# A decoder trunk with product-key experts on one core: more buffers for the gathered v rows

## The chip, the cores and the metric

The kernel runs on one core of a Trainium2 chip. The metric is device time in microseconds of one execution. The runs shown are 1572.21, 1564.13 and 1569.64 us, with a median of 1569.64 us.

## The reference, cut to what matters

The layer has an attention and a recurrent half, and then a product-key expert layer (PEER). Each of 256 tokens picks 16 experts in each of 8 heads out of 16,384. Expert e has a row u[e] and a row v[e], each of 2048 floats:

```
experts = i1 * N_KEYS + i2                       # (token, head, k)
g = softmax(best_s)
act = gelu(einsum('chkd,cd->chk', u_tab[experts], xc))
out = einsum('chk,chkd->cd', g * act, v_tab[experts])
y = rmsnorm(h + out, final_norm_g)
```

## The kernel before, in words

The expert layer is computed densely over u and sparsely over v.

**u stretch.** All 16,384 u rows are multiplied with all tokens; the activations x of the tokens, split in a high and a low part, lie in the tile `xc` (32 KB on each of the 128 partitions). For every expert the activations of the 256 tokens go to a table in DRAM, `wg_d`, and the gates are added there by indirect DMAs (`scatter`, L701). While this runs, VectorE and TensorE make lists of the experts that were picked by at least one token.

**v stretch** (`b_stage`). The picked experts are worked off in 109 tiles of 128 experts. The first two (kind BO) are loaded directly, 107 are gathered: `gather_w` (L895) fetches 128 rows of the table (1 or 2 KB a row, tile `wg`), `gather_v` (L886) fetches the 128 rows of v (8 KB a row, 1 MB in all, tile `vr`). Both are indirect DMAs on GpSimd's queue, in one order. For every tile `ready` makes the weights (`split_w`, VectorE L907 or L909 and what follows it) and splits the v rows into a high part on ScalarE (`vh`, L935 or L938) and a low part on VectorE (`vl`, L936 or L939), in halves of 1024 columns; `multiply` (L951) adds the products of 512 columns into eight PSUM banks. A tile's kind says which token halves it serves: S0 and S1 (one expert of each row used once, so the weight is put into v as a factor: L909, L918, L938, L939) take 8 products, DO 16 (it splits v twice: L907, L912, four L938 and four L939), M0 and M1 12, BO 24 (L907, L935, L936). The kinds are spread evenly; tiles 54 to 64 are DO, S1, BO, BO, M1, S0, S1, BO, M0, DO, BO.

**Buffers.** `vr` and `wg` have five buffers each. In iteration i the program asks for `gather_w(i + 5)`, `gather_v(i + 5)`, `ready(i + 2)` and `multiply(i)`. `gather_v(i + 5)` needs the buffer of tile i, which is free when the split of tile i is done; `gather_w(i + 5)` needs the buffer that `split_w(i)` has read. `vh` and `vl` have eight half buffers each, four tiles of a kind other than DO.

**Order.** A planner puts the instructions of each engine into a fixed order beforehand, by priority (the place in the program) and by when it expects inputs and buffers to be there, so an engine's order is not the program's line by line. A data-dependent branch (`leftovers`, not taken) stands after iteration 1.

**End.** The tile `fin` takes over the place of `xc`: the first four of its 512-column blocks hold the final gain row (`load_fg`, L966), four take the output of token half 0 and four that of half 1. `residual` (L970, SyncE's queue) and `add_residual` add the residual during iterations 4 to 82.

Of the kernel before, what the change touches and what calls it, by code (L numbers as in the profile page):

```python
# [9 lines left out]
F32 = mybir.dt.float32  # L10
# [10 lines left out]
D = 2048  # L21
# [29 lines left out]
ONCE = (S0, DO, S1)  # L51
NT = 107
AHEAD = 5
LOOK = 2
NLEAD = 3
NS1 = 1
# [7 lines left out]
def trunk_kernel(ctx, tc, hT_d, par_d, sink_d, fg_d, win_d, wr_d, wi_d, wout_d, wq_d, sk_d, u_d, v_d, out_d):  # L64
# [31 lines left out]
    box = {}  # L96
# [5 lines left out]
    def at(slot, fn):  # L102
        later.setdefault(slot, []).append(fn)
# [755 lines left out]
    def close_a():  # L859
        ps_x.close()  # L860
        box["bx"] = ExitStack()
        pob = box["bx"].enter_context(tc.tile_pool(name="pob", bufs=1, space=PSUM, reuse_waits="tile"))
        box["o"] = [[pob.tile([128, 512], F32, name=f"oacc{tb}_{q}") for q in range(4)] for tb in range(2)]
        fin = box["xpool"].tile([128, 12, 512], F32, tag="xc", name="fin")
        box["fin"], box["fin2"] = fin[:, 0:8, :], fin[:, 8:12, :]

    tail = [(M1, BASES[M1] + CAPS[M1] - 1 - i) for i in range(3)]
# [4 lines left out]
    order = [(BO, None)] * NLEAD2 + [(k, T_) for _, k, T_ in sorted(spread)] + tail  # L872
# [4 lines left out]
            last_at[tb] = i  # L877

    def gather_v(i):
        raw = box["raw", i] = box["pb"].tile([128, D], F32, tag="vr", name="vr", bufs=5)  # L880
        T_ = order[i][1]
        if T_ is None:
            c = NLIST + i
            nc.sync.dma_start(raw, v_d[128 * c:128 * c + 128, :])
            return
        GP.indirect_dma_start(out=raw, out_offset=None, in_=v_d, in_offset=bass.IndirectOffsetOnAxis(ap=box["iv"][:, T_:T_ + 1], axis=0))  # L886

    def gather_w(i):
        wg = box["wg", i] = box["pb"].tile([128, ROW], F32, tag="wg", name="wg", bufs=5)
        k, T_ = order[i]  # L890
        if T_ is None:
            c = NLIST + i
            nc.sync.dma_start(wg[:, :256], wg_d[1 + 128 * c:129 + 128 * c, 128:384])
            return
        GP.indirect_dma_start(out=wg if k in (DO, BO) else wg[:, :256], out_offset=None, in_=wg_d,  # L895
                              in_offset=bass.IndirectOffsetOnAxis(ap=box["iw"][:, T_:T_ + 1], axis=0),
                              element_offset=256 if k in (S1, M1) else 0)
# [45 lines left out]
    def multiply(w, parts, k, first=(), stop=()):  # L943
        wh, wl = w
        for tb in HALVES[k]:
            for h in range(2):
                vh, vl = parts[2 * tb + h if k == DO else h]
                terms = ((wh, vh), (wh, vl)) if k in ONCE else ((wh, vh), (wh, vl), (wl, vh))
                for n, (a, b) in enumerate(terms):
                    for q in range(2):  # L950
                        PE.matmul(box["o"][tb][2 * h + q], a[:, tb, :], b[:, 512 * q:512 * q + 512],  # L951
                                  start=tb in first and n == 0, stop=tb in stop and n == len(terms) - 1)

    def leftovers():
        n = nc.values_load(box["nov"][0:1, 0:1], min_val=0, max_val=NEXP)
        with tc.If(n > 0):
            with tc.For_i(0, NLIST, 1) as c:
                pb = box["pb"]
                raw = pb.tile([128, D], F32, tag="vr", name="vr", bufs=5)
                wg = pb.tile([128, ROW], F32, tag="wg", name="wg", bufs=5)  # L960
                nc.sync.dma_start(raw, v_d[bass.ds(c * 128, 128), :])
                nc.sync.dma_start(wg, wg_d[bass.ds(c * 128 + 1, 128), :])
                multiply(split_w(wg, BO, box["ovf"][:, bass.ds(c, 1)]), split_v(raw), BO)

    def load_fg():
        nc.sync.dma_start(box["fin"][:, 0:4, :], bass.AP(tensor=fg_d.tensor, offset=fg_d.offset, ap=[[0, 128], [512, 4], [1, 512]]))  # L966

    def residual(k):
        hr = box["hr", k] = box["pb"].tile([128, S], F32, tag="hr", name="hr", bufs=2)
        nc.sync.dma_start(hr, h2_d[:, k, :])  # L970

    def add_residual(k):
        hr = box["hr", k]
        for tb in range(2):
            PE.matmul(box["o"][tb][k // 4][:, (k % 4) * 128:(k % 4) * 128 + 128],  # L975
                      hr[:, tb * 128:tb * 128 + 128], ident, start=False, stop=False)
# [4 lines left out]
    def stats(tb):  # L981
        zz = box["zz", tb] = box["pb"].tile([128, 8], F32, tag="zz", name="zz", bufs=2)
        for q in range(4):
            SC.activation(slot_out(tb, q), box["o"][tb][q], AF.Square, accum_out=zz[:, q:q + 1])  # L984
        V.tensor_reduce(out=zz[:, 4:5], in_=zz[:, 0:4], axis=AX.X, op=ALU.add)
        SC.activation(zz[:, 5:6], zz[:, 4:5], AF.Sqrt, bias=epsc, scale=1.0 / D)  # L986
        V.reciprocal(zz[:, 6:7], zz[:, 5:6])

    def output(tb, q, pool=False, queue=None):
        r = box["zz", tb][:, 6:7]  # L990
        ot = slot_out(tb, q)
        g = box["fin"][:, q, :]
        if pool:
            SC.activation(ot, box["o"][tb][q], AF.Copy, scale=r)
            GP.tensor_tensor(ot, ot, g, ALU.mult)
        else:
            V.scalar_tensor_tensor(ot, box["o"][tb][q], r, g, ALU.mult, ALU.mult)  # L997
        (queue or nc.sync).dma_start(out_d[tb * 128:tb * 128 + 128, q * 512:q * 512 + 512], ot)
# [12 lines left out]
    def ready(i):  # L1011
        if i < len(order):
            box["w", i] = split_w(box.pop(("wg", i)), order[i][0], act=box.pop(("act", i), None))
            box["v", i] = split_v(box.pop(("raw", i)), factors(i))
# [6 lines left out]
    def early_ready(i):  # L1021
        with tc.issue_after(box["hi"].ins), tc.issue_after(box["lo"].ins):
            ready(i)

    def held(fn, i):
        with tc.issue_after(box["ld"].ins):
            fn(i)

    for i in range(AHEAD):
        at(b0 - 10, lambda i=i: held(gather_v, i))  # L1030
        at(b0 - 10 if i < NLEAD2 else b0 - 2, lambda i=i: held(gather_w, i))
    for i in range(LOOK):
        at(b0 - 2 + i, lambda i=i: early_ready(i))

    def b_stage():
        close_a()
        n = len(order)
        for i, (k, _) in enumerate(order):
            if i + AHEAD < n:
                gather_w(i + AHEAD)  # L1040
                gather_v(i + AHEAD)
            ready(i + LOOK)
            multiply(box.pop(("w", i)), box.pop(("v", i)), k, [t for t in range(2) if first_at[t] == i], [t for t in range(2) if last_at[t] == i])
            if i == 1:
                leftovers()
            if i >= 4 and i % 5 == 4 and i // 5 < 16:
                residual(i // 5)
            if i >= 7 and i % 5 == 2 and i // 5 - 1 < 16:
                add_residual(i // 5 - 1)
            if i == 80:  # L1050
                load_fg()
            if i == last_at[0]:
                warm = box["pb"].tile([128, 1], F32, name="warm", bufs=1)
                SC.activation(warm, epsc, AF.Sqrt, scale=0.0)
                stats(0)
                output(0, 0)
                output(0, 1)
                output(0, 2)
                output(0, 3)
        stats(1)  # L1060
        output(1, 0)
        output(1, 1, False, nc.scalar)
        output(1, 2)
        output(1, 3, True, nc.scalar)
# [8 lines left out]
    for i, (src, fn) in enumerate(items):  # L1073
# [9 lines left out]
        for f in later.pop(i, []):  # L1083
            f()
    b_stage()
    box["bx"].close()
    box["wax"].close()
# [58 lines left out]
```

## Time and profile before

| | before |
|---|---|
| runs, us | 1572.21, 1564.13, 1569.64 (median 1569.64) |
| profiled execution, us | 1567.66 |
| its span, first to last instruction, us | 1566.0 |
| TensorE busy | 1541.2 us, 98% |
| VectorE, ScalarE, GpSimd busy | 1270.3, 999.0, 761.2 us |
| DMA | 376.49 MB, mean 240 GB/s |

The profiled execution took 1.66 us more than its span, and it lies 1.98 us below the median of the runs. A busy TensorE is not a TensorE at its peak: products are pipelined and overlap in the records, so missing work shows better in the number of products that start in a window than in busy time. Idle time of an engine costs nothing unless TensorE, or the end, waits for it.

### The profile page before, as it was taken

To read this page: it belongs to the slowest core of one execution; us is meant where nothing else is said; L and a number is where in the kernel's file an instruction comes from. 1 tells how busy PE (TensorE), PEld (TensorE's weight loads), DVE (VectorE), ACT (ScalarE), POOL (GpSimd) and SP (SyncE) were. 2 spreads that over 40 slices of the span, in tenths; PEclk is the share of its full clock that TensorE was granted. 3 is DMA by queue.
4 is the path that set the end of the run, shared out by engine and by line. 5 is a ranking of instruction groups with operands and counts; after the bars stand their busy time and mean duration, and the time that the engine had idled before them with its cause. 6 is when DMAs were issued, how large, how long until landed. Compare 5 with 4: busy or idle time off the path is not lost. (4 is left out here: it accounts for less than half of the span.)

```text
span 1566.0 us, 26985 instructions
## 1 busy us (share of the span) xinstructions
PE 1541.2 (98%) x9361; PEld 1346.6 (86%) x9361; DVE 1270.3 (81%) x2466; ACT 999.0 (64%) x1931; POOL 761.2 (49%) x539
## 2 busy tenths in 40 slices
PE   7999999999999999999999999999999999999997
PEld 6998999999988888888888888888888888887786
DVE  7878788887898998888888787555568899888896
ACT  6676675555556555555555887555567777766786
POOL 2001000000001777877787777774027677887871
PEclk9999999999999999999999999999999999999999
DMA  8997357665576888888887778888869989798895
GB/s 250 271 297 218 109 179 213 201 215 166 184 214 198 213 220 199 191 193 197 195 201 197 196 182 196 211 209 265 253 230 340 380 326 401 287 356 348 328 392 193
DMA packets 188274, 376.49 MB, mean 240 GB/s; under 512 B 51092, under 2 KB 119080, under 8 KB 173928
## 3 DMA queue, kind: packets, MB, share of 16 engines
q1 hardware_dynamic: 93432, 220.93, 46.3%
q0 software_dynamic: 59856, 136.22, 28.6%
q10 hardware_dynamic: 34848, 17.60, 3.9%
q8 instruction: 73, 1.20, 0.3%
q14 instruction: 65, 0.53, 0.1%
HBM read 336.80 MB, written 37.88 MB: 239 GB/s over the span
## 5 line engine op out<-in xcount | busy, mean ns | idle before, releaser
L133 PE MATMUL acc<-xc,hi 128*128 128x512 f32 x2048 | 730.9, 400 | 0.0
L115 ACT ACTIVATE hi<-raw 128x512 fp32r<-128x512 f32 x744 | 463.7, 629 | 385.3 <-PE acc L133 224.2
L117 DVE TENSOR_TENSOR lo<-raw,hi 128x512 fp32r<-128x512 f32 x744 | 507.5, 690 | 202.5 <-ACT hi L115 197.1
L701 POOL DMA_INDIRECT wg_d<-gw,gix x256 | 445.3, 1740 | 311.3 <-ACT hi L115 187.6
L134 PE MATMUL acc<-xc,lo 128*128 128x256 f32 x2048 | 575.1, 281 | 0.2 <-DVE lo L117 0.2
L133 PEld LDWEIGHTS acc<-xc,hi 128*128 128x128 f32 x2048 | 385.0, 188 | 88.1
L134 PEld LDWEIGHTS acc<-xc,lo 128*128 128x128 f32 x2048 | 387.1, 189 | 0.7 <-DVE lo L117 0.5
L895 POOL DMA_INDIRECT wg<-wg_d,iw x107 | 146.7, 1371 | 116.2 <-issue 111.8
L951 PE MATMUL oacc<-vl,wh 128*128 128x512 f32 x632 | 195.8, 392 | 1.2 <-DVE vl L936 0.6
L951 PE MATMUL oacc<-vh,wh 128*128 128x512 f32 x632 | 193.4, 395 | 1.5 <-ACT vh L935 0.8
L886 POOL DMA_INDIRECT vr<-v,iv x107 | 142.7, 1334 | 58.0 <-DVE vl L939 25.1
L939 DVE SCALAR_TENSOR_TENSOR vl<-vr,fac,vh 128x1024 fp32r<-128x1024 f32 x120 | 147.7, 1285 | 16.2 <-ACT vh L938 15.8
L936 DVE TENSOR_TENSOR vl<-vr,vh 128x1024 fp32r<-128x1024 f32 x124 | 147.4, 1219 | 4.3 <-ACT vh L935 4.0
L951 PEld LDWEIGHTS oacc<-vl,wh 128*128 128x128 f32 x632 | 117.6, 188 | 29.4 <-DVE vl L939 4.1
L938 ACT ACTIVATE vh<-vr,fac 128x1024 fp32r<-128x1024 f32 x120 | 129.8, 1141 | 19.2 <-DMA vr<-v,iv 13.4
L951 PEld LDWEIGHTS oacc<-vh,wh 128*128 128x128 f32 x632 | 116.4, 188 | 29.2 <-ACT vh L935 3.3
L935 ACT ACTIVATE vh<-vr 128x1024 fp32r<-128x1024 f32 x124 | 124.9, 1048 | 19.3 <-DMA vr<-v,iv 14.6
L125 PE MATMUL acc<-xgh,hi 128*128 128x256 f32 (+1 forms) x416 | 123.0, 296 | 7.4 <-ACT hi L115 6.4
L127 PE MATMUL acc<-xgh,lo 128*128 128x256 f32 (+1 forms) x416 | 119.7, 288 | 2.4 <-DVE lo L117 2.4
L951 PE MATMUL oacc<-vh,wl 128*128 128x512 f32 x392 | 120.8, 390 | 0.0
L126 PE MATMUL acc<-xgl,hi 128*128 128x256 f32 (+1 forms) x416 | 120.1, 289 | 0.3
L125 PEld LDWEIGHTS acc<-xgh,hi 128*128 128x128 f32 x416 | 79.3, 191 | 12.8 <-ACT hi L115 6.4
(289 smaller groups left out, 2134.9 us busy)
## 6 DMA issues: line engine op xcount, KB each, us to landing
raw<-u SPq DMA_DIRECT2D x256, 512.0 KB
raw<-win SPq DMA_DIRECT2D x52, 512.0 KB
wg_d<-zt SPq DMA_DIRECT2D x128, 128.0 KB
raw<-wout SPq DMA_DIRECT2D x32, 512.0 KB
raw<-wq SPq DMA_DIRECT2D x32, 512.0 KB
wg_d<-at ACTq DMA_DIRECT2D x126, 128.0 KB
wg_d<-gw,gix POOLq DMA_INDIRECT x256, 4.7
h_d<-hT POOLq DMA_DIRECT2D x4, 512.0 KB
```

The source lines that it names most:

```text
L115: box["hi"] = SC.activation(hi, r, AF.Copy)
L117: box["lo"] = V.tensor_tensor(lo, r, hi.bitcast(F32), ALU.subtract)
L125: PE.matmul(acc, hi[:, c], xh[:, k0 + k, :], start=first and k == 0, stop=False)
L133: PE.matmul(acc, hi[:, c], x[:, k0 + k].rearrange("p h t -> p (h t)"), start=first and k == 0, stop=False)
L134: PE.matmul(acc[:, S:], lo[:, c], x[:, k0 + k, 0, :], start=False, stop=last and k == 7)
L701: d = GP.indirect_dma_start(out=flat, out_offset=bass.IndirectOffsetOnAxis(ap=box["ix"][:, tb, j:j + 1], axis=0), in_=box["gw"][:, tb, j:j ...
L886: GP.indirect_dma_start(out=raw, out_offset=None, in_=v_d, in_offset=bass.IndirectOffsetOnAxis(ap=box["iv"][:, T_:T_ + 1], axis=0))
L895: GP.indirect_dma_start(out=wg if k in (DO, BO) else wg[:, :256], out_offset=None, in_=wg_d, in_offset=bass.IndirectOffsetOnAxis(ap=box["i ...
L936: V.tensor_tensor(lo, r, hi.bitcast(F32), ALU.subtract)
L938: SC.activation(hi, r, AF.Copy, scale=fac)
L939: V.scalar_tensor_tensor(lo, r, fac, hi.bitcast(F32), ALU.mult, ALU.subtract)
L951: PE.matmul(box["o"][tb][2 * h + q], a[:, tb, :], b[:, 512 * q:512 * q + 512], start=tb in first and n == 0, stop=tb in stop and n == len( ...
```

## The change

Four more buffers of 1 MB for gathered v rows lie in `fin`, which grows from 12 to 16 blocks of 512 columns (the size of `xc`, so nothing else moves). Of tiles 5 to 95 those with i mod 9 of 5 to 8 (41 tiles) are gathered into these, the others rotate through the five old buffers. `gather_v` for tiles 5 to 8 is issued at the beginning of `b_stage`, and iteration i asks for `gather_v(i + 9)` instead of `gather_v(i + 5)`. `gather_w` still runs five tiles ahead with five buffers. Tiles 96 to 108 use the five old buffers only. As the gain row's place is now the first of the late buffers, `load_fg` moves from iteration 80 to iteration 100.

```diff
--- before.py
+++ after.py
@@ -51,6 +51,7 @@
 ONCE = (S0, DO, S1)
 NT = 107
 AHEAD = 5
+DEEP = 9
 LOOK = 2
 NLEAD = 3
 NS1 = 1
@@ -861,7 +862,8 @@
         box["bx"] = ExitStack()
         pob = box["bx"].enter_context(tc.tile_pool(name="pob", bufs=1, space=PSUM, reuse_waits="tile"))
         box["o"] = [[pob.tile([128, 512], F32, name=f"oacc{tb}_{q}") for q in range(4)] for tb in range(2)]
-        fin = box["xpool"].tile([128, 12, 512], F32, tag="xc", name="fin")
+        fin = box["xpool"].tile([128, 16, 512], F32, tag="xc", name="fin")
+        box["late"] = [fin[:, 4 * j:4 * j + 4, :].rearrange("p a n -> p (a n)") for j in range(4)]
         box["fin"], box["fin2"] = fin[:, 0:8, :], fin[:, 8:12, :]
 
     tail = [(M1, BASES[M1] + CAPS[M1] - 1 - i) for i in range(3)]
@@ -877,7 +879,10 @@
             last_at[tb] = i
 
     def gather_v(i):
-        raw = box["raw", i] = box["pb"].tile([128, D], F32, tag="vr", name="vr", bufs=5)
+        if i >= AHEAD and i % DEEP >= AHEAD and i < len(order) - 13:
+            raw = box["raw", i] = box["late"][i % DEEP - AHEAD]
+        else:
+            raw = box["raw", i] = box["pb"].tile([128, D], F32, tag="vr", name="vr", bufs=5)
         T_ = order[i][1]
         if T_ is None:
             c = NLIST + i
@@ -1035,10 +1040,13 @@
     def b_stage():
         close_a()
         n = len(order)
+        for i in range(AHEAD, DEEP):
+            gather_v(i)
         for i, (k, _) in enumerate(order):
             if i + AHEAD < n:
                 gather_w(i + AHEAD)
-                gather_v(i + AHEAD)
+            if i + DEEP < n:
+                gather_v(i + DEEP)
             ready(i + LOOK)
             multiply(box.pop(("w", i)), box.pop(("v", i)), k, [t for t in range(2) if first_at[t] == i], [t for t in range(2) if last_at[t] == i])
             if i == 1:
@@ -1047,7 +1055,7 @@
                 residual(i // 5)
             if i >= 7 and i % 5 == 2 and i // 5 - 1 < 16:
                 add_residual(i // 5 - 1)
-            if i == 80:
+            if i == 100:
                 load_fg()
             if i == last_at[0]:
                 warm = box["pb"].tile([128, 1], F32, name="warm", bufs=1)
```

## Rows read from the trace of the kernel before

**Rows 1.** From the page's part 4, the chain of waits that ended last: shares of the span by engine, tile and line.

```profile
PE oacc L951 14%; DMA vr<-v,iv 2%; POOL vr L886 2%; DMA wg<-wg_d,iw 1%; POOL wg L895 1%; DVE vl L939 0%; ACT vh L935 0%; PE oacc L975 0%; DVE fin L997 0%; ACT fin L984 0%; DVE vl L936 0%; ACT vh L938 0%; DVE w L909 0%; ACT L986 0%; DVEq L1142 0%
```

**Rows 2.** The matrix products of the v stretch on TensorE, grouped by form. Columns: line, engine, operation and tiles, count: shortest, median and longest ns, first and last start in us, forms.

```profile
L951 PE MATMUL oacc<-vh,wh x632: 387/389/502, 1165.2 to 1554.7; 128*128 128x512 f32 x158
L951 PE MATMUL oacc<-vh,wl x392: 387/389/398, 1166.2 to 1556.5; 128*128 128x512 f32 x196
L975 PE MATMUL oacc<-ident,hr x64: 270/274/276, 1197.7 to 1467.6; 128*128 128x128 f32 x64
```

**Rows 3.** TensorE's timeline, two rows between which 34 products stand in pairs, unbroken. Columns: start us, length us, engine, line, operation, tiles, count in the row.

```profile
1347.47 0.62 PE L951 MATMUL oacc<-vh,wh 128*128 128x512 f32 x2
...
1355.18 0.61 PE L951 MATMUL oacc<-vh,wh 128*128 128x512 f32 x2
```

**Rows 4.** TensorE in windows of 10 us, the products of L951 alone. Columns: window, its length, busy us and starts (x), granted clock, DMA share, GB/s of the core's DMA. A window with four residual transposes beside them holds 44 products when nothing is missing (1195 to 1205 is one), one without holds 46.

```profile
1195.00:1205.00 10.00, 9.80 (x44) 1.00 0.98 373
1235.00:1245.00 10.00, 10.00 (x46) 1.00 1.02 411
...
1375.00:1385.00 10.00, 9.60 (x42) 1.00 1.01 405
...
1415.00:1425.00 10.00, 9.24 (x37) 1.00 0.95 350
1425.00:1435.00 10.00, 9.75 (x38) 1.00 1.02 416
...
1465.00:1475.00 10.00, 9.46 (x37) 1.00 1.01 414
1475.00:1485.00 10.00, 9.70 (x40) 1.00 1.02 414
...
1535.00:1545.00 10.00, 10.00 (x46) 1.00 0.57 214
```

**Rows 5.** The waits of the v stretch (1157 to 1566 us): who waited for whom, us in total, times, longest.

```profile
POOL vr L886 <- DVE vl L939: 25.1, 18, 3.0
...
ACT vh L935 <- DMA vr<-v,iv: 14.6, 8, 3.8
ACT vh L938 <- DMA vr<-v,iv: 13.4, 8, 5.4
...
DVE w L909 <- DMA wg<-wg_d,iw: 11.2, 8, 4.8
DVE w L907 <- DMA wg<-wg_d,iw: 9.2, 7, 3.2
```

**Rows 6.** GpSimd's timeline: the gathers around one long one, and two more long ones. In brackets: idle time before, and what ended it.

```profile
1359.34 1.74 POOL L886 DMA_INDIRECT vr<-v,iv  x1 [1.79 <-DVE vl L939]
1361.38 9.79 POOL L895 DMA_INDIRECT wg<-wg_d,iw  x1 [0.30 <-issue]
1371.47 0.94 POOL L886 DMA_INDIRECT vr<-v,iv  x1 [0.30 <-issue]
1372.72 0.95 POOL L895 DMA_INDIRECT wg<-wg_d,iw  x1 [0.31 <-issue]
...
1403.63 9.72 POOL L895 DMA_INDIRECT wg<-wg_d,iw  x1 [0.30 <-issue]
...
1452.85 9.45 POOL L886 DMA_INDIRECT vr<-v,iv  x1 [0.61 <-DVE vl L939]
```

**Rows 7.** VectorE's timeline from that long gather on.

```profile
1368.00 2.35 DVE L936 TENSOR_TENSOR vl<-vr,vh 128x1024 fp32r<-128x1024 f32 x2
1373.07 0.29 DVE L909 TENSOR_TENSOR w<-wg 128x128 f32<-128x128 f32 x1 [2.72 <-DMA wg<-wg_d,iw]
...
1377.85 0.42 DVE L907 TENSOR_TENSOR w<-wg 128x256 f32<-128x256 f32 x1 [1.96 <-DMA wg<-wg_d,iw]
1378.44 2.48 DVE L939 SCALAR_TENSOR_TENSOR vl<-vr,fac,vh 128x1024 fp32r<-128x1024 f32 x2 [0.16 <-ACT vh L938]
...
1382.09 0.33 DVE L909 TENSOR_TENSOR w<-wg 128x128 f32<-128x128 f32 x1 [0.79 <-DMA wg<-wg_d,iw]
```

**Rows 8.** ScalarE's timeline of the same time.

```profile
1377.25 2.20 ACT L938 ACTIVATE vh<-vr,fac 128x1024 fp32r<-128x1024 f32 x2 [3.45 <-DMA vr<-v,iv]
...
1381.64 2.01 ACT L935 ACTIVATE vh<-vr 128x1024 fp32r<-128x1024 f32 x2 [1.90 <-DMA vr<-v,iv]
```

**Rows 9.** DMA in a window of 2 us inside that gather. Columns: window, its length, GpSimd busy us (instructions), granted clock, DMA share, GB/s.

```profile
1368.00:1370.00 2.00, 2.00 (x1) 1.00 0.00 0
```

**Rows 10.** A place where the same VectorE operation and the gathers overlap: one row of VectorE's timeline, one of GpSimd's.

```profile
1235.04 2.35 DVE L936 TENSOR_TENSOR vl<-vr,vh 128x1024 fp32r<-128x1024 f32 x2
...
1235.91 1.16 POOL L886 DMA_INDIRECT vr<-v,iv  x1 [0.30 <-issue]
```

**Rows 11.** The start of the stretch: GpSimd's timeline, one row of VectorE's, and a window of 20 us (columns: busy us and starts of PE, weight load, DVE, ACT, POOL, then clock, DMA share, GB/s).

```profile
1168.72 1.02 POOL L895 DMA_INDIRECT wg<-wg_d,iw  x1 [1.25 <-DVE w L907]
...
1177.82 0.43 DVE L907 TENSOR_TENSOR w<-wg 128x256 f32<-128x256 f32 x1 [1.17 <-DMA wg<-wg_d,iw]
...
1160.00:1180.00 20.00, 19.85 (x93) 16.03 (x93) 15.27 (x25) 13.24 (x22) 11.89 (x12) 1.00 0.83 275
```

**Rows 12.** SyncE's queue: the gain row's load, then the residual loads.

```profile
1165.44 0.33 SPq L966 DMA_DIRECT2D fin<-fg  x1
1198.36 232.02 SPq L970 DMA_DIRECT2D hr<-h_d  x14
```

## The prediction

> **What bounds the kernel now.** I read the chain of waits first. It does not run through one engine: besides the products (L951, 14% of the span) it holds the gathers' landings and their issue on GpSimd, 2 + 2 + 1 + 1% [rows 1]. So the v stretch is near a balance between TensorE and the stream of gathers, and the question is how much TensorE loses to that stream. Busy time can't say it; counts can. The first v product starts at 1165.2 us, the last at 1556.5, and with its 0.39 us the stretch takes 391.7 us [rows 2]. Where nothing is missing, 34 products start in 7.71 us, one each 0.2268 us [rows 3]. The 1656 products (632 + 632 + 392, the middle form as often as the first, since each product with vh has one with vl) need 375.6 us at that pace. Four residual transposes cost two products' places (44 a window instead of 46 [rows 4]), 0.45 us, and there are 64 [rows 2], so 7.3 us. 391.7 - 375.6 - 7.3 = 8.8 us is all that a perfect supply of v and w could give back, 0.56% of the run. What a measurement of this kernel can tell from no change is about 0.5%, 7.85 us of 1569.64.
>
> The windows say where it goes: 2 products are missing in 1375 to 1385, 9 and 6 in 1415 to 1435, 7 and 6 in 1465 to 1485; 30 in all, 6.8 us [rows 4]. After that nothing is missing.
>
> The cause is one step earlier. A gather normally holds GpSimd for 0.95 us; those that began at 1361.38, 1403.63 and 1452.85 held it 9.79, 9.72 and 9.45 us [rows 6], and inside the first the DMA fell to 0 GB/s [rows 9]. Each of the three losses follows one of these. During the first, VectorE ran through the splits that it had data for, went dry at 1368.00 + 2.35 = 1370.35 and waited 2.72 us for w [rows 7]. GpSimd's own waits for a free v buffer come to 25.1 us [rows 5]: the stream is now and then stopped by the five buffers.
>
> **The change part by part.** What is added is lead for v alone. The waits that it can remove are ScalarE's for v, 14.6 + 13.4 = 28.0 us; VectorE's for w, 11.2 + 9.2 = 20.4 us, stay unless w comes earlier [rows 5]. The decisive point is whether v or w is late, and the timelines answer it tile by tile. The long gather at 1361.38 is w of tile 60 (kinds S0, S1, BO, M0, DO for 59 to 63): L909 at 1373.07 reads it, L907 at 1377.85 reads w of tile 61, L909 at 1382.09 w of 62 [rows 7]. v of tile 60 is the next gather, 1371.47, and w of 61 follows at 1372.72 [rows 6]. ScalarE gets v of 60 at 1377.25, VectorE w of 61 at 1377.85, 0.6 us later; v of 61 at 1381.64, w of 62 at 1382.09, 0.45 us later [rows 7, 8]. Both come out of one queue, in the order of issue. And VectorE's fixed order has w of tile 61 (1377.85) ahead of the low split of tile 60 (L939, 1378.44) [rows 7]. So v of 60 is late, but w of 61 is late just behind it, and the split waits for both.
>
> After the change the place of v of 60 in GpSimd's queue is taken by v of 64, the same 1 MB, and w of 61 still stands behind it: w has five buffers and the same lead as before. What is gained there is what VectorE waited beyond w: 0.16 us at 1378.44 [rows 7], and at most the 0.6 us between v and w, some ten tiles over the three recoveries. That is 1.6 to 6 us on VectorE; the bounds on the path are nothing (the next w takes it back) and 6.8 us (all of the loss). I take 1.5 us, near the row's 0.16, because w stays late.
>
> The start. Four more gathers go out at once, 4 x (0.95 + 0.30) = 5.0 us of GpSimd and 4.2 MB. They can't begin before the last u product has read `xc`, just before 1165.2. In 1160 to 1180 the DMA moved 275 GB/s [rows 11] where it reaches 405 to 416 [rows 4]: room for 2.6 to 2.8 MB, and the gain row's 1 MB no longer loads there [rows 12]. So 0.4 to 0.6 MB, 1.0 to 1.5 us, finds no room. VectorE already waits 1.17 us there for the w that was issued at 1168.72 [rows 11], and now more v data are ahead of such a w. Below, nothing (the products of three BO tiles give TensorE a cover of 3 x 24 x 0.2268 = 16.3 us); above, the whole 4.2 MB, 10.4 us at 405 GB/s, less the 3.7 us from that wait's end at 1177.8 to 1165.2 + 16.3 = 1181.5, when TensorE has worked off that cover: 6.7. I take 0.7, half of what finds no room.
>
> The steps that cost nothing: the 41 tiles in `fin` need the same ScalarE and VectorE work, covered as now; a longer `fin` has the size of `xc`. `load_fg` now waits for the split of tile 95. In the present order SyncE issued it before all residual loads, though it stands behind them in the program [rows 12]: the planner goes by readiness, so the residuals need not wait behind it. Its 1 MB is 2.6 us of DMA; in 1535 to 1545 the DMA is 0.57 busy and no product is missing [rows 4]. If that cover were gone, the gain row would come late at the end, at 2.6 us at most. From tile 96 on v falls back to five buffers, as now, where now nothing is lost; nothing taken.
>
> Sum against the profiled execution: 1567.66 + 0.7 - 1.5 = 1566.9 us. The median lies 1.98 us higher, which makes 1568.8 us.
>
> **A rule weighed.** The row is that the DMA stood at 0 GB/s while GpSimd sat 9.79 us in one gather, and that the gather went on 0.95 us before 1371.17, at 1370.2, when VectorE ran dry (1370.35) [rows 6, 7, 9]. The Trainium skill, page "SBUF — State Buffer", section "SBUF: two separate sides", names such a case: a VectorE operation that holds the port pair it shares with GpSimd keeps GpSimd from writing descriptors for its DMAs, so the DMA engines sit idle though nothing contends for them. By that rule no number of v buffers shortens a lockout, and lockouts would grow if more v let VectorE work without a gap; that is the slower rival below, and by the rule alone the sum would be that rival's. The trace agrees for the three long gathers and not everywhere: at 1235.91 a gather took 1.16 us beside the same VectorE operation [rows 10].
>
> **The rivals.** *v's lead is worth what it looks like.* Before a lockout four more tiles of v lie ready, and with v there earlier the planner may put the split of a tile ahead of the next tile's w. That would give w one tile more, some 391.7 / 109 = 3.6 us, against VectorE's waits of 2.72, 1.96 and 0.79 us [rows 7]. For it: 28.0 us of waits for v against 20.4 for w [rows 5]. Against it: the pairs above. It gives back 3 to 8 us, most likely 5: 1564.6 us, and 1561 at best.
>
> *Lockouts come more often.* GpSimd went on when VectorE ran dry [rows 6, 7]; if VectorE never waits for v, it runs dry less often. The three late lockouts cost 6.8 / 3 = 2.3 us of TensorE each, beyond the four tiles of split v that stand between. From the third extra one on the time is over 0.5% longer; four to six more give 9 to 14 us: 1578 to 1583 us. For it: it is the end of the first one as the rows show it. Against it: while GpSimd fills four more buffers it waits less for VectorE, and two of the three gathers follow such a wait [rows 6]; and a VectorE with enough v waits for TensorE instead, which makes gaps.
>
> *The start costs more.* If w of tiles 5 to 7 lands behind all four megabytes, 3 to 6.7 us: 1572.6 to 1576.3 us. For it: VectorE has no slack for w there (1.17 us of waiting [rows 11]). Against it: the room of some 3.6 MB worked out above.
>
> *The change does not do what it says.* The planner may hold the later v gathers to the rhythm of w, so that v is nine ahead in the program and hardly more than five on the chip. That too gives 1569 to 1570 us, and I put it with the forecast.
>
> **How the numbers follow.** No change within 3 us, 0.56; v's lead pays 3 to 8 us, 0.24; more lockouts, 0.13; a dear start, 0.07. The likeliest gives 1568.8 us. Faster by over 0.5% needs nearly all of the 8.8 us: a third of the second case, 0.08. Slower by over 0.5%: most of the third case, 0.10. The rest, 0.82, is the same. The range for 8 in 10 leaves out the best of the second case and the worse half of the third: 1562 to 1576 us; the forecast's own is 1566 to 1572.
>
> **What would show it.** Right: ScalarE's waits for v fall from 28 us to a few, VectorE's for w stay near 20 us, long gathers stay, and after each one VectorE's next instruction waits for w while v lies ready. The missing products after them stay near 30. GpSimd's waits for a free v buffer shrink before 1300 us. Wrong: windows with 46 products throughout (v's lead was all that mattered), waits for w well under 20 us, more than three gathers over 9 us, or a stretch that starts with missing products before 1200 us.

## The result, and the profile after

The changed kernel is slower: 1592.19, 1586.77 and 1589.99 us, beside 1570.62 us for the kernel before (median of four: the three runs shown ahead and one of 1571.60); the ratio is 1.0126, 95% interval 1.0087 to 1.0164. (A fourth run of 5361.24 us stands apart and is not in the ratio.) Forecast were 1568.8 us and 1562 to 1576. The profiled execution took 1592.19 us, the longest of the three; its span is 1590.3. The lines of the changed kernel stand five further: L951 is L956, L909 is L914, L939 is L944.

The products by form answer to [rows 2]:

```profile
L956 PE MATMUL oacc<-vh,wh x632: 387/389/796, 1167.1 to 1577.8; 128*128 128x512 f32 x158
L956 PE MATMUL oacc<-vh,wl x392: 387/389/507, 1168.0 to 1581.3; 128*128 128x512 f32 x196
```

The stretch takes 1581.3 + 0.39 - 1167.1 = 414.6 us where it took 391.7. It holds the same 375.6 + 7.3 = 382.9 us of work, so 31.7 us are lost in it, where 8.8 were. The windows of TensorE, products of L956 alone, as in [rows 4]:

```profile
1185.00:1195.00 10.00, 9.02 (x37) 1.00 1.00 409
1195.00:1205.00 10.00, 9.51 (x39) 1.00 0.94 349
...
1285.00:1295.00 10.00, 8.70 (x36) 1.00 0.20 60
...
1485.00:1495.00 10.00, 8.02 (x31) 1.00 0.57 230
...
1515.00:1525.00 10.00, 5.76 (x21) 0.86 0.90 347
1525.00:1535.00 10.00, 10.00 (x37) 0.80 0.59 186
...
1555.00:1565.00 10.00, 9.13 (x38) 1.00 0.76 284
```

Against 46 (44 where transposes stand between) the start lacks 9 and 5, single windows in the middle up to 15, and from 1515 us on the end is thin: 25 in one window and 9 in the next. A part of these 34 goes with the clock. TensorE stands for 4.14 us before 1522.85, and from 1522.2 to 1529.0 us its granted clock is 0.50, the lower of its two levels (1.2 and 2.4 GHz). Once TensorE works again, 13 products start in the 6.15 us up to 1529.0; at the full pace there is room for 27. Whether their parts would have been ready for that is not shown. The waits, as in [rows 5]:

```profile
ACT w L924 <- DVE w L914: 50.7, 25, 2.5
DVE vl L944 <- ACT vh L943: 43.4, 30, 1.7
...
DVE w L914 <- DMA wg<-wg_d,iw: 6.8, 2, 5.5
DVE w L912 <- DMA wg<-wg_d,iw: 6.1, 1, 6.1
...
ACT vh L940 <- DMA vr<-v,iv: 3.9, 1, 3.9
```

ScalarE waits 3.9 us for v (28.0 before), VectorE 12.9 us for w (20.4 before). The change does what it says, and fewer waits for data go with more time. What grew are waits of the two engines for each other: VectorE for the high part 43.4 us, ScalarE for the S kinds' product 50.7 us. The kernel before had these:

```profile
ACT w L919 <- DVE w L909: 28.3, 17, 3.3
...
DVE vl L939 <- ACT vh L938: 15.8, 15, 1.7
```

Why, is seen in VectorE's timeline before the window with 31 products, and in ScalarE's:

```profile
1473.07 0.28 DVE L914 TENSOR_TENSOR w<-wg 128x128 f32<-128x128 f32 x1
1473.27 0.22 DVE L923 TENSOR_SCALAR wh<-wg 128x128 fp32r<-128x128 f32 x1
1475.07 2.48 DVE L944 SCALAR_TENSOR_TENSOR vl<-vr,fac,vh 128x1024 fp32r<-128x1024 f32 x2 [1.58 <-ACT vh L943]
1477.46 0.28 DVE L914 TENSOR_TENSOR w<-wg 128x128 f32<-128x128 f32 x1
...
1479.40 2.48 DVE L944 SCALAR_TENSOR_TENSOR vl<-vr,fac,vh 128x1024 fp32r<-128x1024 f32 x2 [1.52 <-ACT vh L943]
...
1486.70 4.87 DVE L944 SCALAR_TENSOR_TENSOR vl<-fin,fac,vh 128x1024 fp32r<-128x1024 f32 x4 [1.60 <-ACT vh L943]
1491.49 0.41 DVE L912 TENSOR_TENSOR w<-wg 128x256 f32<-128x256 f32 x1
```

```profile
1473.44 0.31 ACT L924 ACTIVATE w<-w 128x128 f32<-128x128 f32 x1 [2.39 <-DVE w L914]
1473.66 0.18 ACT L924 ACTIVATION_READ_ACCUMULATOR w<-w 128x1 f32 x1
1473.88 2.20 ACT L943 ACTIVATE vh<-vr,fac 128x1024 fp32r<-128x1024 f32 x2
1477.78 0.31 ACT L924 ACTIVATE w<-w 128x128 f32<-128x128 f32 x1 [1.71 <-DVE w L914]
```

TensorE then waits for the parts of the last of these tiles:

```profile
1486.72 0.73 PE L956 MATMUL oacc<-vh,wh 128*128 128x512 f32 x2 [0.58 <-ACT vh L943]
```

A tile of kind S0 or S1 is a chain over two engines: product on VectorE (L914), factor on ScalarE (L924), high part with that factor on ScalarE (L943), low part on VectorE (L944). If VectorE makes the product of tile i+1 ahead of the split of tile i, ScalarE works off its part meanwhile. Here VectorE makes it only when the split of tile i is done, and then waits 1.5 to 1.6 us for the answer, in all three S and DO tiles shown. From 1473.07 to 1491.49 VectorE needs 18.4 us for four tiles (S, S, M, DO; 4.7 us of it these three waits) whose 8 + 8 + 12 + 16 products take TensorE 44 x 0.2268 = 10.0 us. That eats the store of tiles split ahead, and 15 products, 3.4 us, are missing in the window. (The three waits are a part of it: without them VectorE would still need 13.7 us for these four.)

In VectorE's fixed order of instructions the product of tile i+1 stood ahead of the split of tile i for 76 of the 109 tiles before the change, and for 14 after it (counted in the two traces); the planner has turned the order. That was the first theory (**order**). The end gave a rival (**tail**): VectorE stands 6.07 us for the w of tile 94,

```profile
1520.55 0.42 DVE L912 TENSOR_TENSOR w<-wg 128x256 f32<-128x256 f32 x1 [6.07 <-DMA wg<-wg_d,iw]
```

and GpSimd's queue has v of tiles 95, 96 and 97 (asked for nine ahead, the last two out of the five old buffers, and waiting for one) in front of the w of tiles 92, 93 and 94:

```profile
1491.84 9.45 POOL L891 DMA_INDIRECT fin<-v,iv  x1 [3.04 <-DVE vl L944]
1501.60 0.95 POOL L900 DMA_INDIRECT wg<-wg_d,iw  x1 [0.30 <-issue]
1504.80 0.94 POOL L891 DMA_INDIRECT vr<-v,iv  x1 [2.26 <-DVE w L914]
1506.04 0.95 POOL L900 DMA_INDIRECT wg<-wg_d,iw  x1 [0.30 <-issue]
1509.13 6.16 POOL L891 DMA_INDIRECT vr<-v,iv  x1 [2.15 <-DVE vl L944]
1515.60 0.94 POOL L900 DMA_INDIRECT wg<-wg_d,iw  x1 [0.30 <-issue]
```

The waits for one of the five buffers are only 2.26 and 2.15 us here; the two gathers of 9.45 and 6.16 us, where 0.95 is usual, hold the queue for another 13.7. What the tail theory says is that the small w gathers stand behind all of this.

And the **start**: four v gathers go out between 1167.53 and 1173.12 us, the next w behind them, and VectorE waits 5.46 us for a w (1.17 in [rows 11]):

```profile
1183.75 0.29 DVE L914 TENSOR_TENSOR w<-wg 128x128 f32<-128x128 f32 x1 [5.46 <-DMA wg<-wg_d,iw]
```

### The profile page after: what moved, and what is told of

It is laid out like the page before. It is cut to its first block, busy times and chain, and to the rows that moved or that the text cites. A ratio compares the mean times of both kernels' runs of the same rounds, so it can differ in the third digit from the quotient of the medians.

```text
span 1590.3 us, 26989 instructions
## 1 busy us (share of the span) xinstructions
PE 1551.3 (98%) x9361; PEld 1344.9 (85%) x9361; DVE 1268.3 (80%) x2466; ACT 998.5 (63%) x1931; POOL 766.6 (48%) x539
## 4 chain that ended last, share of the span: by engine, by line
PE 79%; DVE 7%; ACT 4%; issue 4%; DMA 3%; POOL 1%; SPq 0%; DVEq 0%; ACTq 0%; POOLq 0%
PE acc L134 29%; PE acc L135 15%; PE oacc L956 10%; PE acc L126 7%; PE acc L127 6%; PE acc L128 6%; DVE vl L944 2%; DVE vl L941 2%; ACT vh L943 2%; DMA wg<-wg_d,iw 1%; PE aux L722 1%; PE aux L421 1%; DMA hT<-hT 1%; POOL wg L900 1%; PE aux L802 1%
## 5 line engine op out<-in xcount | busy, mean ns | idle before, releaser
L135 PEld LDWEIGHTS acc<-xc,lo 128*128 128x128 f32 x2048 | 386.5, 189 | 0.0
L956 PE MATMUL oacc<-vh,wh 128*128 128x512 f32 x632 | 199.6, 401 | 10.9 <-ACT vh L943 7.7
L956 PE MATMUL oacc<-vl,wh 128*128 128x512 f32 x632 | 198.0, 395 | 2.9 <-DVE vl L944 2.0
L900 POOL DMA_INDIRECT wg<-wg_d,iw x107 | 126.7, 1184 | 107.6 <-issue 107.0
L956 PEld LDWEIGHTS oacc<-vh,wh 128*128 128x128 f32 x632 | 116.1, 190 | 45.4 <-ACT vh L943 14.0
L956 PEld LDWEIGHTS oacc<-vl,wh 128*128 128x128 f32 x632 | 117.5, 189 | 34.3 <-DVE vl L944 7.1
L891 POOL DMA_INDIRECT vr<-v,iv x66 | 102.6, 1554 | 56.2 <-DVE vl L944 19.2
L956 PE MATMUL oacc<-vh,wl 128*128 128x512 f32 x392 | 121.4, 391 | 1.2 <-DVE wl L930 1.2
L944 DVE SCALAR_TENSOR_TENSOR vl<-vr,fac,vh 128x1024 fp32r<-128x1024 f32 x74 | 90.9, 1281 | 32.1 <-ACT vh L943 24.2
L941 DVE TENSOR_TENSOR vl<-vr,vh 128x1024 fp32r<-128x1024 f32 x78 | 94.0, 1215 | 0.3 <-ACT vh L940 0.3
L956 PEld LDWEIGHTS oacc<-vh,wl 128*128 128x128 f32 x392 | 73.3, 188 | 18.0 <-DVE wl L930 2.3
L128 PEld LDWEIGHTS acc<-xgh,lo 128*128 128x128 f32 x416 | 78.9, 190 | 3.5 <-DVE lo L118 3.2
```

The lines of the kernel that those rows point to most:

```text
L128: PE.matmul(acc, lo[:, c], xh[:, k0 + k, :], start=False, stop=last and k == 7)
L135: PE.matmul(acc[:, S:], lo[:, c], x[:, k0 + k, 0, :], start=False, stop=last and k == 7)
L941: V.tensor_tensor(lo, r, hi.bitcast(F32), ALU.subtract)
L944: V.scalar_tensor_tensor(lo, r, fac, hi.bitcast(F32), ALU.mult, ALU.subtract)
```

## The experiments

Ratios are to the kernel before on the same chip; medians are compared only where runs shared a chip.

**The order forced, first try.** In the changed kernel `ready(i)` makes all weights of tile i+1 first, and the split of tile i is issued behind the last VectorE instruction of these.

```diff
-            box["w", i] = split_w(box.pop(("wg", i)), ...)
-            box["v", i] = split_v(box.pop(("raw", i)), factors(i))
+            make_w(i)                       # does nothing where it was made before
+            make_w(i + 1)
+            with tc.issue_after(box["wd"].ins):   # its last VectorE instruction
+                box["v", i] = split_v(box.pop(("raw", i)), factors(i))
```

> The changed kernel with one thing added: VectorE's order is forced to make the weights of tile i+1 before it splits v of tile i, for every tile. Before the change the planner had it so for 76 of 109 tiles, after it for 14. Theory order (the planner's new order makes VectorE and ScalarE wait for each other in every tile): VectorE's waits for ScalarE's high part, 43.4 us after and 15.8 before, fall to 16 or less, the products that are missing before 1485 us come back, and of the 20.5 us that the change lost at least 10 come back: 1575 to 1581 us. Theory tail (v gathers of tiles from 96 on stand in GpSimd's queue ahead of the w gathers that are needed first): the waits fall, but the end is as late: 1586 to 1591 us, with the missing products still between 1485 and 1580 us.

Measured: 1589.82 us, ratio 1.0151 (1.0111 to 1.0191). The number is the tail theory's, but the run doesn't decide. VectorE's waits for the scaled `vh` did go (none is left of the 43.4 us), but the edit made a new wait of the same kind, in the tiles with a low weight part:

```profile
DVE wl L930 <- ACT wh L929: 55.3, 51, 2.5
```

`wl` needs ScalarE's `wh`; put ahead of the split as a whole, the weights make VectorE wait there.

**The tail undone.**

```diff
+            if i + AHEAD < n and i + AHEAD >= n - 13:
+                gather_v(i + AHEAD)
-            if i + DEEP < n:
+            if i + DEEP < n - 13:
                 gather_v(i + DEEP)
```

> The changed kernel with one thing undone: v of tiles 96 to 108, which use the five old buffers, is asked for five tiles ahead as before the change, right behind the w of the same tile, not nine ahead; GpSimd's queue then alternates w, v to its end. Theory tail: the wait of 6 us for w of tile 94 and the low windows from 1485 us on go, some 67 missing products of 0.2268 us, 15 us: 1575 to 1579 us. Theory order: the tail is as thin as before it because VectorE and ScalarE still wait for each other (43 us): 1586 to 1591 us.

Measured: 1582.29 us, ratio 1.0112 (1.0056 to 1.0169). The time doesn't decide: it lies between the two forecasts, the four runs go from 1578.25 to 1593.05 us, and the ratio can't be told from the changed kernel's 1.0126. The windows do: 1515 to 1525 us holds 44 products where the changed kernel has 21, but 1185 to 1195 still has 34. The long gather is still there (9.44 us at 1491.42), but the w of tiles 92 to 96 now go out right behind it, and VectorE waits for no w at the end. So the tail is a cost, and not the whole; its price comes from a pair of runs further on.

```profile
1185.00:1195.00 10.00, 8.73 (x34) 1.00 0.97 369
...
1515.00:1525.00 10.00, 9.93 (x44) 1.00 0.80 326
```

**Both.**

> Both edits of the two runs above in the changed kernel. If order and tail are separate costs that add up, this comes to the time of the kernel before, 1570 us or a little less (1565 to 1572). If one of the two is the whole cause, this is no better than the better one of them. If the longer lead itself costs something that neither touches (the late start of the stretch, 2 us, and lockouts of GpSimd), 1574 to 1580 us.

Measured: 1587.18 us, ratio 1.0121 (1.0083 to 1.0159). By its letter this is the second case, no better than the tail alone; but the forced order's own wait for `wh` (57.8 us here) is in it, as in the first try, from which it differs by 2.6 us on the same chip. So it told only that this was the wrong order to force.

**The kernel before with the order turned.** Five buffers and the old gathers; only VectorE's weights of a tile are held behind the split of the tile ahead.

```diff
+                with tc.issue_after(box["vd"].ins):   # last split instruction of tile i-1
+                    box["w", i] = split_w(...)
```

> The kernel before, with five buffers for v, and VectorE's order forced the other way: the weights of a tile are made only after the split of the tile ahead of it (106 of 109 tiles; the changed kernel has 89 such and 6 later ones). Theory order: VectorE's waits for ScalarE rise from 15.8 us to 40 or more, and the time by 8 to 20 us: 1579 to 1590 us. Theory tail: v and w come as before, the products that VectorE holds back are covered by the four tiles of split v: 1568 to 1573 us.

Measured: 1602.57 us, ratio 1.0214 (1.0174 to 1.0255). With nothing else changed the turned order costs more than the whole change, and the same wait grows as in the changed kernel, and further; here the order is turned for all tiles:

```profile
DVE vl L939 <- ACT vh L938: 79.5, 46, 6.8
```

**The order put right in the changed kernel.** Now only the product of tile i+1, one VectorE instruction, is held ahead of the split of tile i.

```diff
+    def mult_w(wg, k, act=None):            # the first VectorE instruction of split_w, alone
...
+            make_w(i + 1)                   # mult_w of tile i + 1
+            box["w", i] = split_w(..., w=box.pop(("wm", i)))
+            with tc.issue_after(box["wd"].ins):
+                box["v", i] = split_v(box.pop(("raw", i)), factors(i))
```

> The changed kernel with VectorE's order forced as the planner mostly had it before: only the product of gate and activation for tile i+1 (one instruction) stands ahead of the split of tile i; the low part of the weights, which waits for ScalarE and cost 55 us of waiting in the first order that was tried, stays free. Theory order: VectorE's waits for ScalarE's vh and wh together fall under 25 us (after: 43.4 for vh alone), the windows with 34 and 35 products about 1277 and 1487 us become full, and the time falls from 1591 to 1578 to 1582 us (the end stays thin). Theory that the order is not a cause in the changed kernel: 1588 to 1592 us.

Measured: 1573.57 us, ratio 1.002 (0.9997 to 1.0044), better than expected. 1.06% of the time (the ratios 1.0126 and 1.002), some 17 us, came back by the place of one instruction a tile. GpSimd's queue has the same order of gathers as in the changed kernel from w of tile 6 to v of tile 95, so it is not the queue that was mended there. VectorE's waits for the scaled `vh` are down to 2.2 us, those of `wl` for `wh` come to 20.2. Left are the start, with 41 products in 10 us, and the end, where VectorE now waits 14.89 us at once for a w (that of tile 102, behind v of tiles 102 to 105) and two windows of 10 us hold 13 and 30 products:

```profile
DVE vl L952 <- ACT vh L951: 2.2, 2, 1.2
...
1533.86 0.42 DVE L910 TENSOR_TENSOR w<-wg 128x256 f32<-128x256 f32 x1 [14.89 <-DMA wg<-wg_d,iw]
```

**The order and the tail.**

> The same order, and v of tiles 96 to 108 asked for five tiles ahead as before. If order and tail are separate causes they add: the tail alone gave 1582 from 1591, and the order takes its 8 to 12 us: 1568 to 1575 us; what is left over the kernel before is then the start, some 3 us of products missing between 1187 and 1197 us. If they cover each other: 1578 to 1582 us.

Measured: 1565.76 us, ratio 0.9953 (0.9931 to 0.9976), 7.8 us less than without the tail's edit on the same chip: the two add up, and somewhat more came back than expected.

**And the start.**

```diff
-        for i in range(AHEAD, DEEP):
-            gather_v(i)
+        nv = AHEAD
...
+            while nv < n - 13 and nv <= min(i + DEEP, 2 * i + AHEAD + 1):
+                gather_v(nv)
+                nv += 1
```

> The same, and the start undone too: v of tiles 5 to 8 is not asked for in one go; each of the first iterations asks for two v tiles behind its w, until the lead is nine. Theory start (w of tile 5 to 7 stands behind four megabytes of v): the window about 1187 to 1197 us, with 32 to 34 products, fills to 44 or more, 2.5 to 3 us less than the run without this edit: 1566 to 1572 us. If v's lead is worth something by itself, this is where it shows: 1558 to 1564 us. Else the start is not the gathers' but the order's: no change against the run without this edit.

Measured: 1560.49 us, ratio 0.9922 (0.9898 to 0.9947), 5.3 us less than the run before it. The window 1185 to 1195 goes from 36 products to 46, 2.3 us; first the run without the ramp, then this one:

```profile
1185.00:1195.00 10.00, 9.26 (x36) 1.00 1.00 396
```

```profile
1185.00:1195.00 10.00, 10.00 (x46) 1.00 0.98 358
```

The rest is not the window's own: the run without the ramp also lacked some 24 products, 5.4 us, behind gathers of 9.31 us at 1193.22 and of 10.83 us at 1230.88, which this run does not have. That the ramp took these two away is seen in one trace of each run; why it did is not shown. The v stretch takes 1550.1 + 0.39 - 1167.1 = 383.4 us, 0.5 us over its 382.9 us of products and transposes (and 7.3 us less than without the ramp, though it begins 1.7 us later):

```profile
L964 PE MATMUL oacc<-vh,wh x632: 387/389/478, 1167.1 to 1549.2; 128*128 128x512 f32 x158
...
L964 PE MATMUL oacc<-vh,wl x392: 388/389/393, 1168.1 to 1550.1; 128*128 128x512 f32 x196
```

**The order alone, without more buffers.** The kernel before with the product forced ahead for all tiles.

> The kernel before, five buffers, with the order forced the same way for all 109 tiles in place of 76. Theory order: 33 tiles less wait for ScalarE (15.8 us of waiting before, some of it on the way to TensorE): 1562 to 1568 us where the kernel before has 1565 to 1571. If the free order was good because it fell back to the other one when w was late: 1570 to 1576 us.

Measured: 1563.48 us, ratio 0.9954 (0.9934 to 0.9974), on the chip of the three runs above. The stretch is 1551.2 + 0.39 - 1165.1 = 386.5 us:

```profile
L959 PE MATMUL oacc<-vh,wh x632: 388/389/502, 1165.1 to 1547.5; 128*128 128x512 f32 x158
...
L959 PE MATMUL oacc<-vh,wl x392: 388/389/398, 1166.1 to 1551.2; 128*128 128x512 f32 x196
```

So of the 8.8 us that supply could give back, 5.2 are had by order with five buffers, and v's longer lead, with the tail and the start mended, adds 3.0 us (1563.48 - 1560.49; the runs of the two, 1559.07 to 1561.35 and 1561.98 to 1566.78, do not overlap).

**Tail and start without the order.**

> The changed kernel with the tail undone and v's lead built up two tiles an iteration at the start, as in the best run so far, but with VectorE's order left to the planner (tile i+1's product ahead of the split of tile i for 11 tiles, further ahead for 4). Theory start as a cost of its own: the window about 1187 to 1197 us fills from 33 to 44 products, and 1582 becomes 1577 to 1579.5 us. Theory order alone (that window is thin because of the ping-pong between ScalarE and VectorE, not because of the gathers): the window keeps 32 to 36 products, 1581 to 1584 us.

Measured: 1576.65 us, ratio 1.0043 (1.002 to 1.0066). The start is a cost of its own: the window fills without the order's help. VectorE's waits for `vh` stay at 51.4 us. Against the run with the order too (0.9922, on another chip), the order is worth 1.2% here.

```profile
1185.00:1195.00 10.00, 10.00 (x45) 1.00 1.02 419
```

**What makes the long gathers.** In the kernel before, L936 is written with L939's operation and a factor of 1.

```diff
-                V.tensor_tensor(lo, r, hi.bitcast(F32), ALU.subtract)
+                V.scalar_tensor_tensor(lo, r, 1.0, hi.bitcast(F32), ALU.mult, ALU.subtract)
```

> The kernel before, and all engines' orders as before; only the low split of the kinds without a factor (L936, 124 instructions of 1.218 us) is written as the operation with a factor (L939's, 1.280 us) with a factor of 1. VectorE gets 7.7 us more work. In the kernel before all long gathers on GpSimd begin beside L936. Theory lockout by that operation: no gather over 3.5 us is left (7 before, of 3.83 to 9.79 us), the thin windows about 1375, 1415 to 1435 and 1465 to 1485 us fill, and the time falls by 3 to 7 us: 1563 to 1567. Theory that the long gathers are not made by this operation: 5 or more of them stay, and the time is 1569 to 1574 us.

Measured: 1566.55 us, ratio 0.9991 (0.9962 to 1.0019), and seven gathers over 3.5 us, three of them of 9.78 to 9.98. The time lies in the first theory's range, but by the ratio nothing changed, and as many long gathers as before stayed: the rewritten form does not take them away. (The expectation is wrong where it has all seven of the kernel before begin beside L936: three do, the other four begin as L939 ends, beside L907, L909 or L925.) GpSimd's row, and VectorE's around it:

```profile
1223.77 9.86 POOL L895 DMA_INDIRECT wg<-wg_d,iw  x1 [0.31 <-issue]
```

```profile
1221.37 2.48 DVE L939 SCALAR_TENSOR_TENSOR vl<-vr,fac,vh 128x1024 fp32r<-128x1024 f32 x2
1223.77 0.29 DVE L909 TENSOR_TENSOR w<-wg 128x128 f32<-128x128 f32 x1
...
1232.52 0.29 DVE L925 TENSOR_TENSOR wl<-w,wh 128x128 fp32r<-128x128 f32 x1
1236.10 0.43 DVE L907 TENSOR_TENSOR w<-wg 128x256 f32<-128x256 f32 x1 [3.29 <-DMA wg<-wg_d,iw]
```

The gather begins as VectorE leaves L939, and ends, the 0.95 us that a gather takes anyway taken off, at 1232.68, as VectorE goes dry at 1232.81. Another one goes on with no gap in VectorE, at 1275.88 + 6.77 - 0.95 = 1281.70, as L939 begins:

```profile
1275.88 6.77 POOL L886 DMA_INDIRECT vr<-v,iv  x1 [1.79 <-DMA vr<-v,iv]
```

```profile
1281.62 0.22 DVE L918 TENSOR_SCALAR wh<-wg 128x128 fp32r<-128x128 f32 x1
1281.75 2.47 DVE L939 SCALAR_TENSOR_TENSOR vl<-vr,fac,vh 128x1024 fp32r<-128x1024 f32 x2
```

Of the 14 gathers over 3.5 us in this trace and in that of the kernel before, 11 end, taken so, within 0.2 us of one or the other: 8 as VectorE goes dry, 3 as L939 begins. From its beginning to that end VectorE starts no L939 in any of the 14. L939 differs from the rewritten L936 only in that its factor is a column of `fac` and not a constant. Why that lets GpSimd go on stays open.

**Nine buffers, the lead of five.**

```diff
-        for i in range(AHEAD, DEEP):
-            gather_v(i)
...
-            if i + DEEP < n:
-                gather_v(i + DEEP)
+            if i + AHEAD < n:
+                gather_v(i + AHEAD)
```

> The changed kernel with its nine v buffers, but v asked for five tiles ahead, as w is, not nine. The planner then keeps VectorE's order as in the kernel before: the product of tile i+1 ahead of the split of tile i for 76 tiles (14 in the changed kernel). Theory order (the lead is what makes the planner turn the order, and the turned order is the cost): the time of the kernel before, 1565 to 1571 us, with VectorE's waits for ScalarE at 20 us or less. Theory that nine buffers in this place cost by themselves (late gain row, the place of the buffers): 1576 to 1591 us.

Measured: 1566.37 us, ratio 0.9961 (0.9934 to 0.9987). Buffers, their place and the late gain row cost nothing; this is faster than the kernel before by 0.4%.

**Nine buffers, a lead of six** (the loop at the start asks for tile 5 alone, the iteration for i + 6).

> The same with v asked for six tiles ahead, one more than w. In VectorE's order the product of tile i+1 then stands ahead of the split of tile i for 18 tiles. Theory order: one tile of lead turns the order and costs most of what the whole change cost: VectorE's waits for ScalarE 40 to 55 us, 1577 to 1584 us (the end, where GpSimd's queue alternates w and v here, and the start are not thin). Theory that the cost grows with the lead (gathers of v ahead of w in GpSimd's queue): 1568 to 1574 us.

Measured: 1573.29 us, ratio 1.0017 (0.9992 to 1.0042), 6.9 us more than the run above on the same chip. One tile of lead turns the order, and VectorE's wait triples. First lead five, then lead six:

```profile
DVE vl L944 <- ACT vh L943: 12.8, 12, 1.7
```

```profile
DVE vl L944 <- ACT vh L943: 40.3, 30, 1.7
```

The wait came out as the order theory had it; the time, below its 1577 to 1584, fell into the range of the rival. Some 40 us of such waits cost 7 us here and 17 to 19 us at a lead of nine: how much of a wait on VectorE reaches TensorE is not shown by the runs (it may depend on what the tiles around it leave in store). So the turned order is shown as a cost at each lead, and why it costs more at the longer one is open.

## Why the prediction was wrong

*The ceiling was right.* 8.8 us was put as all that supply could give back, and the best run gave back 8.3 of it (391.7 - 383.4), though not by supply alone: 5.2 came by VectorE's order with five buffers. The change lost 22.9 us of stretch instead. By the stretches of the profiles, in the order in which they were mended: the order 414.6 - 396.7 = 17.9 us, the tail 396.7 - 390.7 = 6.0, start and the long gathers 390.7 - 383.4 = 7.3. These are single executions, and the shares hang on which is mended first: the tail alone, mended first, shortens the stretch by 10.8 us (414.6 to 403.8).

*The step that failed most: the order taken as given.* The working read "VectorE's fixed order has w of tile 61 (1377.85) ahead of the low split of tile 60", and used it only for who is late. That order was itself the planner's, made from when it expects v and w; the change moves v alone. The rival "v's lead is worth what it looks like" even named the turn (the planner "may put the split of a tile ahead of the next tile's w") and priced it as a gain for w of 3.6 us. The sign was wrong: what the early product buys is not time for w's gather, but the time that ScalarE needs between product and split. A wait of 15.8 us stood in the waits for it (L939 for L938), and was not among the rows; it is the one that went to 43.4. The turn's price, 1.06 to 1.2% where measured within the changed kernel, is larger than everything in the sum.

*The term that was nothing: the tail.* "From tile 96 on v falls back to five buffers, as now" was true of the buffers and not of the queue. Before, v of tile i+5 was asked for when its buffer was about to come free. Now the request stands nine tiles early in an in-order queue, waits there for one of five buffers, and the w behind it waits too, also when such a v meets a long gather (6.16 us at 1509.13); TensorE stands, and its clock falls. With the order right, undoing this gave 7.8 us.

*The start.* Taken as 0.7 us, with a rival at 3 to 6.7. The window lost 9 products beside 46, and mending it gave 10 products, 2.3 us, or 5.3 us with what followed. VectorE's wait for w there rose from 1.17 to 5.46 us: the rival had the mechanism, and products missing before 1200 us were one of the prediction's own signs of being wrong.

*w late behind v.* The waits for w were to stay near 20 us; they fell to 12.9, of which 11.5 are one wait at the start and one at the end, and with the order right v's lead is worth 3.0 us, where 1.5 were taken and 3 to 8 given to the rival: twice what was taken, and the low end of the rival's. The turned order hid it.

*Lockouts.* Nine gathers over 3.5 us instead of seven, one over 9 instead of three: they did not come more often in a way that matters, but the longest one (9.45 us at 1491.84) stands in front of the thin end. The rule of the Trainium skill (page "SBUF — State Buffer", section "SBUF: two separate sides"), that a VectorE operation with two SBUF inputs holds the port pair against a GpSimd operation that reads SBUF for the whole instruction, is not decided by the rewritten split, which has two such inputs as well. But L939 has two too, and 3 long gathers ended as it began: by that rule, if a gather counts as reading SBUF (its indices lie there), L939 should have held them on.

*load_fg and the longer `fin`* cost nothing, as said: the run with nine buffers and a lead of five has both, and is faster than before.

## What to carry to other kernels

Where a planner makes the order from expected times, moving one stream ahead of another is also an edit of every engine's order: compare the two orders, count the pairs that have turned, and look for a chain that goes over two engines and back. Of a request that is moved earlier in an in-order queue ask, at each place where the buffers are fewer than its lead, what will stand behind it while it waits; and let a lead grow step by step at the start. Here the gain, 0.8% over the kernel before, needed one instruction's place, the old rhythm for the last 13 tiles, and a ramp; without the first, the lead of nine cost time (ratio 1.0043).

## What the runs showed of the hardware

The long gathers begin beside other forms of VectorE's work than the one under suspicion (9.86 us at 1223.77 with the split rewritten), and 11 of 14 end where VectorE runs dry or begins L939. What they cost differs: a gather of 6.63 us at 1278.26 in the best run stands in a stretch that lost 0.5 us in all, while those of 9.31 and 10.83 us in the run without the ramp, with the same order, stand before 24 missing products, 5.4 us.

TensorE's granted clock fell to 0.50 (1.2 GHz) for 6.8 us in the changed kernel, after TensorE had stood for 4.14 us before 1522.85.
